# Gate-matrix one-hots in a Trainium2 block: two tokens side by side in place of eight

## Chip, core and metric

The kernel runs as one program on one core of a Trainium2 chip. The core has five engines with a queue each: TensorE (PE; its weight loads are shown apart as PEld), VectorE (DVE), ScalarE (ACT), GpSimd (POOL) and SyncE (SP), which here only issues DMAs. The metric is the device time of one execution in microseconds. A profile gives the span from the first to the last instruction of one execution.

## What is computed

The reference is one transformer block on 512 latent tokens of width 1024 (with 256 context tokens): two recurrent token mixers, a merge, and a product-key mixture of experts ("PEER"). Only the last part is touched:

```python
q = (t @ w_query).reshape(n_tok, P_HEADS, 2, P_DQ)
sc = jnp.einsum('thcd,hckd->thck', q, sub_keys)
s1, i1 = lax.top_k(sc[:, :, 0], P_TOPK)
s2, i2 = lax.top_k(sc[:, :, 1], P_TOPK)
cand = (s1[..., :, None] + s2[..., None, :]).reshape(n_tok, P_HEADS, P_TOPK * P_TOPK)
top_s, top_i = lax.top_k(cand, P_TOPK)
e1 = jnp.take_along_axis(i1, top_i // P_TOPK, axis=-1)
e2 = jnp.take_along_axis(i2, top_i % P_TOPK, axis=-1)
experts = (e1 * P_NKEYS + e2)
gates = jax.nn.softmax(top_s, axis=-1)
...
act = jax.nn.gelu(jnp.einsum('td,tkd->tk', tb, expert_u[eb])) * gb
return jnp.einsum('tk,tkd->td', act, expert_v[eb])
```

There are 8 heads with 16 picks each, so 128 experts per token, out of 128 x 128.

## The kernel before

**Two ways for the tokens.** The 512 tokens are four blocks of 128. Block 0 fetches its 128 experts per token by indirect DMA (helper `gather`: one gather of 128 rows of 4 KB and one VectorE step on it, 256 times in all). Blocks 1 to 3 go through all 16384 experts with dense matmuls: `side_u(e)` loads one tile of `u` (512 KB), splits it into a high and a low part (`whi` on ScalarE, `wlo` on GpSimd or VectorE) and makes 24 matmuls (lines 99 to 101 of `mm3`, 128 weights columns against 384 token columns, into `pS`); later the same is done with `v`, weighted by a dense gate matrix `G[token, e1, e2]`.

**The gate matrix.** `routing(b)` for b = 1, 2, 3 makes that matrix for 128 tokens. For each token the matrix is a product of two one-hot matrices over the 128 picks: `oh1[:, 0]` holds (e1 == column) and `oh2` holds (e2 == column) times the gate, the gate in two fp16 parts (z = 0, 1). Picks lie on partitions. The loop over `tg` (16 tokens) and `t8` (8 tokens) is one round per 8 tokens, 16 rounds per block, 48 in all. One round is:

- VectorE, line 1228: `oh1` = (iota == index) for both indices, 128 partitions x 2048 fp16;
- VectorE, line 1229: `oh2` = second half of `oh1` times the gate parts, 2048 fp16;
- TensorE, line 1235: 16 pairs of a weight load (128 columns of `oh1` or `oh2`) and a matmul over 128 columns, two per token, into two PSUM banks `pg_` of four tokens;
- ScalarE, line 1237: two evictions of 128x512 into `st`;
- SyncE, line 1238: per two rounds, 1 MB of `st` to DRAM (`GD`).

The lines of the operands before:

```python
sel = pR.tile([128, 2, 128], F16, name="sel", bufs=2)
oh1 = pR.tile([128, 2, 128, 8], F16, name="oh1", tag="oh", bufs=4)
oh2 = pR.tile([128, 2, 128, 8], F16, name="oh2", tag="oh", bufs=4)
V.tensor_tensor(oh1, twice(io8), over(sel, ts), op=OP.is_equal)
held[0] = V.tensor_tensor(oh2, twice(oh1[:, 1]), over(ghl, ts), op=OP.mult)
T.matmul(pg_[:, q_], oh1[:, 0, :, t], oh2[:, z, :, t], start=z == 0, stop=z == 1)
```

Tokens are the innermost dimension (8 fp16 = 16 bytes), so both TensorE operands of one token step 8 elements, 16 bytes, from one column to the next. VectorE's operand `sel` or `ghl` is a run of 8 elements that is read 128 times over.

**What sets the order.** The generators `routing(b)` and `us()` are woven by `weave` (15 steps of routing to 20 tiles of `u`), and the build then schedules the instructions of each engine by its own cost estimates, so a change of shapes can move instructions between their neighbours. All engines take their queue in order. The four buffers of tag `oh` are two rounds: `oh1` of a round can be written when the matmuls of the round two before are done. `wraw` has two buffers, `whi` and `wlo` three each, `gr` five, `gst` two. `held` ties each gather's VectorE step behind the last VectorE step of the stage. One block's work thus has an index stretch (top-k, no gate matmuls) and a gate stretch (16 rounds).

## Time and profile before

| | |
|---|---|
| device time, median of 3 runs | 3078.58 us (3072.75 to 3085.27) |
| span of the profiled execution | 3060.6 us |
| median less span | 18.0 us |
| busy share PE / DVE / ACT / POOL | 94% / 60% / 37% / 36% |
| three gate stretches | 109.6 + 108.3 + 107.0 = 324.9 us |

The page has the span of the profiled execution and no device time of its own for it; the 18.0 us are the distance of that span to the runs' median. The gate stretches run from the first one-hot of a block to its last gate matmul: 1744.6 to 1854.2, 1906.5 to 2014.8 and 2068.1 to 2175.1 us. [...] A matmul's shown length is longer than its distance to the next, since matmuls are pipelined; distances between starts are the measure.

### The profile page before, as it was taken

The page shows a single profiled execution, that of the slowest core. Times are in us where ns is not written, and L with a number is a line of the kernel's source. Part 1 is how long each engine was busy: PE and PEld are TensorE (multiplying, and loading weights), DVE is VectorE, ACT ScalarE, POOL GpSimd, SP SyncE. Part 2 cuts the span into 40 slices and gives each one's busy share as a digit, 9 for nine tenths or more (in the row PEclk, how much of TensorE's full clock was granted, in tenths as well). Part 3 has the DMA queues.
Part 4 walks back from the last instruction along what each step waited for, and adds up shares of the span by engine and source line. Part 5 has one row for each costly group of instructions (what it writes and reads, how often), then busy time and mean ns, then how long its engine had stood idle before and what let it go on. Part 6 is the DMA issues. An engine that isn't in the chain of part 4 may idle for free.

```text
span 3060.6 us, 40793 instructions
## 1 busy us (share of the span) xinstructions
PE 2875.4 (94%) x15664; PEld 2277.6 (74%) x15664; DVE 1848.8 (60%) x3273; ACT 1122.3 (37%) x1647; POOL 1100.0 (36%) x674
## 2 busy tenths in 40 slices
PE   6899999999999999999999799999999999999998
PEld 3777667766776666667788678787888888887776
DVE  6555455455453567734578957455577766666668
ACT  3433323333332555515223244434333333333333
POOL 2313223232220222200003625252466655655665
PEclk9999999999999989999999788898899999999999
DMA  5323223232232323326423656564788888878885
GB/s 204 98 67 90 67 70 95 75 86 77 83 83 68 112 81 104 100 89 204 158 92 109 199 184 207 185 212 155 252 289 283 294 279 273 291 280 286 285 279 195
DMA packets 243732, 507.92 MB, mean 166 GB/s; under 512 B 56736, under 2 KB 125760, under 8 KB 239440
## 3 DMA queue, kind: packets, MB, share of 16 engines
q1 hardware_dynamic: 206672, 371.07, 37.5%
q0 software_dynamic: 36864, 134.23, 12.4%
q8 instruction: 123, 2.02, 0.3%
q14 instruction: 73, 0.60, 0.1%
HBM read 440.37 MB, written 64.86 MB: 165 GB/s over the span
## 4 chain that ended last, share of the span: by engine, by line
PE 34%; DMA 10%; DVE 6%; issue 2%; ACT 2%; POOL 1%; SPq 0%; ACTq 0%; DVEq 0%; POOLq 0%
DMA wraw<-in_u_t 6%; PE pS L101 4%; PE pS L99 4%; PE pS L100 4%; PE oacc L100 3%; DMA wraw<-in_v_rows 3%; PE oacc L101 3%; PE oacc L99 3%; DVE wlo L95 2%; ACT whi L94 1%; PE pq L99 1%; PE pq L101 1%; PE pq L100 1%; DVE gscr L1098 1%; PE psc L1132 0%
## 5 line engine op out<-in xcount | busy, mean ns | idle before, releaser
L94 ACT CAST whi<-wraw 128x1024 fp32r<-128x1024 f32 x384 | 402.9, 1050 | 893.3 <-DMA wraw<-in_v_rows 225.8
L95 DVE TENSOR_TENSOR wlo<-wraw,whi 128x1024 fp32r<-128x1024 f32 x333 | 491.1, 1475 | 328.0 <-ACT whi L94 321.9
L99 PE MATMUL pS<-tTh,whi 128*128 128x384 f32 x1024 | 377.8, 369 | 36.1 <-ACT whi L94 24.3
L101 PE MATMUL pS<-tTh,wlo 128*128 128x384 f32 x1024 | 374.6, 366 | 10.7 <-POOL wlo L95 6.6
L100 PE MATMUL pS<-tTl,whi 128*128 128x384 f32 x1024 | 373.5, 365 | 0.0
L99 PE MATMUL oacc<-whi,ah 128*128 128x512 f32 x768 | 302.8, 394 | 16.1 <-ACT ah L1281 16.1
L100 PE MATMUL oacc<-wlo,ah 128*128 128x512 f32 x768 | 304.2, 396 | 2.7 <-DVE wlo L95 2.6
L101 PE MATMUL oacc<-whi,al 128*128 128x512 f32 x768 | 303.6, 395 | 0.9 <-DVE al L1282 0.9
L99 PE MATMUL pcl<-hTh,whi 128*128 128x512 f32 x704 | 301.1, 428 | 0.0
L1277 POOL TENSOR_TENSOR ag<-af,gread 128x384 f32<-128x384 f32 x128 | 224.4, 1753 | 211.8 <-DVE al L1282 201.1
L101 PE MATMUL pcl<-hTh,wlo 128*128 128x512 f32 x704 | 292.0, 415 | 0.0
L100 PE MATMUL pcl<-hTl,whi 128*128 128x512 f32 x704 | 290.9, 413 | 0.0
L99 PEld LDWEIGHTS pS<-tTh,whi 128*128 128x128 f32 x1024 | 215.4, 210 | 45.6 <-ACT whi L94 27.2
L95 POOL TENSOR_TENSOR wlo<-wraw,whi 128x1024 fp32r<-128x1024 f32 x51 | 125.8, 2469 | 313.5 <-ACT whi L94 219.8
L1095 POOL DMA_INDIRECT gr<-in_u_rows,eidx x128 | 178.7, 1396 | 142.9 <-DVE gscr L1098 101.2
L101 PEld LDWEIGHTS pS<-tTh,wlo 128*128 128x128 f32 x1024 | 214.4, 209 | 16.2 <-POOL wlo L95 7.9
L100 PEld LDWEIGHTS pS<-tTl,whi 128*128 128x128 f32 x1024 | 214.3, 209 | 3.3
L1095 POOL DMA_INDIRECT gr<-in_v_rows,eidx x128 | 191.6, 1497 | 67.1 <-DVE gacc L1102 46.9
L99 PEld LDWEIGHTS oacc<-whi,ah 128*128 128x128 f32 x768 | 146.2, 190 | 47.6 <-ACT ah L1281 18.8
L100 PEld LDWEIGHTS oacc<-wlo,ah 128*128 128x128 f32 x768 | 146.1, 190 | 35.1 <-DVE wlo L95 5.7
L101 PEld LDWEIGHTS oacc<-whi,al 128*128 128x128 f32 x768 | 145.9, 190 | 33.2 <-DVE al L1282 2.9
L1098 DVE SCALAR_TENSOR_TENSOR gscr<-gr,ttk 128x1024 bf16<-128x1024 f32 x128 | 169.5, 1324 | 0.7
(1197 smaller groups left out, 5462.5 us busy)
## 6 DMA issues: line engine op xcount, KB each, us to landing
wraw<-in_u_t SPq DMA_DIRECT2D x128, 512.0 KB, 4.4
wraw<-in_v_rows SPq DMA_DIRECT2D x128, 512.0 KB, 4.7
wraw<-in_w_c SPq DMA_DIRECT2D x88, 512.0 KB, 3.7
GD<-gst SPq DMA_DIRECT2D x24, 1024.0 KB, 4.2
gread<-GD SPq DMA_DIRECT2D x16, 1536.0 KB, 12.9
bw<-in_w_ada SPq DMA_DIRECT2D x64, 256.0 KB, 2.9
afD<-afx SPq DMA_DIRECT2D x56, 192.0 KB, 3.6
af<-afD SPq DMA_DIRECT2D x56, 192.0 KB, 4.7
```

The source lines that it names most:

```text
L94: S.copy(hi, raw)
L95: (eng or V).tensor_tensor(lo, raw, hi.bitcast(F32), op=OP.subtract)
L99: T.matmul(o, Lh, Rh, start=first, stop=False)
L100: T.matmul(o, Lh, Rl, start=False, stop=False)
L101: T.matmul(o, Ll, Rh, start=False, stop=last)
L1095: G.indirect_dma_start(out=r, out_offset=None, in_=A["u_rows" if i < NSEL else "v_rows"], in_offset=IndirectOffsetOnAxis(ap=eidx[:, n:n + ...
L1098: x = V.scalar_tensor_tensor(scr, r, 1.0, ttk, op0=OP.mult, op1=OP.mult, accum_out=gs[:, n:n + 1])
L1277: G.tensor_tensor(ag.rearrange("p (g t) -> p g t", t=GT), af.rearrange("p (g t) -> p g t", t=GT), gr[:, :, e % EG, :], op=OP.mult)
```

## The change

The innermost dimension of the one-hots goes from 8 tokens to 2. `oh1` and `oh2` are now [128, 8, 128, 2]: of the 8 slabs of `oh1`, 0 to 3 are e1 and 4 to 7 are e2 for token pairs; the slabs of `oh2` are the two gate parts. TensorE's operands step 2 elements (4 bytes) from column to column. `io8` becomes `io2` (256 elements in place of 1024); `sel` is stored per 8 tokens so that one operand covers e1 and e2, which ScalarE's copy writes in that order. `oh2`, which was one instruction of 2048 elements, becomes two of 1024. Comment lines are removed as well; that part of the diff is left out here.

```diff
-            io8 = pR.tile([128, 128, 8], F16, name="io8")
-            G.iota(io8, pattern=[[1, 128], [0, 8]], base=0, channel_multiplier=0, allow_small_or_imprecise_dtypes=True)
+            io2 = pR.tile([128, 128, 2], F16, name="io2")
+            G.iota(io2, pattern=[[1, 128], [0, 2]], base=0, channel_multiplier=0, allow_small_or_imprecise_dtypes=True)
...
-                sel = pR.tile([128, 2, 128], F16, name="sel", bufs=2)
+                sel = pR.tile([128, 16, 2, 8], F16, name="sel", bufs=2)
...
-                S.copy(sel, pt3[:, 0:2])
+                S.copy(sel.rearrange("p g z t -> p z g t"), pt3[:, 0:2].rearrange("p z (g t) -> p z g t", t=8))
...
-                def over(ap, ts):
-                    """[p, 2, t] -> [p, 2, 128, 8]"""
-                    return ap[:, :, None, ts].to_broadcast([128, 2, 128, 8])
-
-                def twice(ap):
-                    return ap[:, None].to_broadcast([128, 2, 128, 8])
+                def over(ap):
+
+                    n = ap.shape[1] // 2
+                    return ap.rearrange("p (t u) -> p t u", u=2)[:, :, None, :].to_broadcast([128, n, 128, 2])
...
-                        oh1 = pR.tile([128, 2, 128, 8], F16, name="oh1", tag="oh", bufs=4)
-                        oh2 = pR.tile([128, 2, 128, 8], F16, name="oh2", tag="oh", bufs=4)
-                        V.tensor_tensor(oh1, twice(io8), over(sel, ts), op=OP.is_equal)
-                        held[0] = V.tensor_tensor(oh2, twice(oh1[:, 1]), over(ghl, ts), op=OP.mult)
+                        oh1 = pR.tile([128, 8, 128, 2], F16, name="oh1", tag="oh", bufs=4)
+                        oh2 = pR.tile([128, 8, 128, 2], F16, name="oh2", tag="oh", bufs=4)
+                        V.tensor_tensor(oh1, io2[:, None].to_broadcast([128, 8, 128, 2]),
+                                        over(sel[:, (tg * GT + t8) // 8].rearrange("p z t -> p (z t)")),
+                                        op=OP.is_equal)
+                        for z in range(2):
+                            held[0] = V.tensor_tensor(oh2[:, 4 * z:4 * z + 4], oh1[:, 4:8], over(ghl[:, z, ts]),
+                                                      op=OP.mult)
...
-                                    T.matmul(pg_[:, q_], oh1[:, 0, :, t], oh2[:, z, :, t], start=z == 0, stop=z == 1)
+                                    T.matmul(pg_[:, q_], oh1[:, t // 2, :, t % 2], oh2[:, 4 * z + t // 2, :, t % 2],
+                                             start=z == 0, stop=z == 1)
```

The build also moves instructions. On TensorE, at the first two rounds of the first gate stretch (`oh_13688` and `oh_13689` are the first round's one-hots, `pg` its banks, `pS` the matmuls of `side_u`), before:

```order
L1235 MATMUL pg__13702<-oh_13689,oh_13688 128x128
L99 MATMUL pS<-tTh,whi 128x384
L100 MATMUL pS<-tTl,whi 128x384
L101 MATMUL pS<-tTh,wlo 128x384
L99 MATMUL pS<-tTh,whi 128x384
L100 MATMUL pS<-tTl,whi 128x384
L101 MATMUL pS<-tTh,wlo 128x384
L99 MATMUL pS<-tTh,whi 128x384
L100 MATMUL pS<-tTl,whi 128x384
L1235 LDWEIGHTS oh_13712
L1235 MATMUL pg__13716<-oh_13713,oh_13712 128x128
```

And now (line 1237 is the line that was 1235):

```order
L1237 MATMUL pg__13703<-oh_13689,oh_13688 128x128
L101 MATMUL pS<-tTh,wlo 128x384
L99 MATMUL pS<-tTh,whi 128x384
L1237 LDWEIGHTS oh_13713
L1237 MATMUL pg__13718<-oh_13714,oh_13713 128x128
L1237 LDWEIGHTS oh_13713
L1237 MATMUL pg__13728<-oh_13714,oh_13713 128x128
L101 MATMUL pS<-tTh,wlo 128x384
L99 MATMUL pS<-tTh,whi 128x384
L1237 LDWEIGHTS oh_13713
L1237 MATMUL pg__13718<-oh_13714,oh_13713 128x128
```

Most rounds are now split: their first two pairs (the first pair of each bank) stand two or three `pS` matmuls ahead of the other fourteen. The number of gate pairs and of `pS` matmuls is the same.

On VectorE, at the same place (`io` is the iota, `gscr` the step on a gathered row, `pos`, `top_s` and `c` belong to block 2's top-k), before:

```order
L1228 TENSOR_TENSOR oh_13688<-io_11931,sel 128x2048
L1213 SCALAR_TENSOR_TENSOR ghl<-pt_13678,ghl 128x128
L1161 MAX top_s<-c_14537 128x8
L1229 TENSOR_TENSOR oh_13689<-oh_13688,ghl 128x2048
L1228 TENSOR_TENSOR oh_13712<-io_11931,sel 128x2048
L1162 MAX_INDEX pos<-top_s,c_14537 128x8
L1229 TENSOR_TENSOR oh_13713<-oh_13712,ghl 128x2048
L1098 SCALAR_TENSOR_TENSOR gscr,gs<-gr,ttk 128x1024
L1228 TENSOR_TENSOR oh_13775<-io_11931,sel 128x2048
```

And now:

```order
L1226 TENSOR_TENSOR oh_13688<-io_11931,sel 128x2048
L1213 SCALAR_TENSOR_TENSOR ghl<-pt_13678,ghl 128x128
L1230 TENSOR_TENSOR oh_13689<-oh_13688,ghl 128x1024 x2
L1226 TENSOR_TENSOR oh_13713<-io_11931,sel 128x2048
L1161 MAX top_s<-c_14553 128x8
L1230 TENSOR_TENSOR oh_13714<-oh_13713,ghl 128x1024 x2
L1098 SCALAR_TENSOR_TENSOR gscr,gs<-gr,ttk 128x1024
L1226 TENSOR_TENSOR oh_13777<-io_11931,sel 128x2048
```

The sequence stays; the gate product is two instructions, and small top-k steps move by a place. The gathers on GpSimd, the evictions on ScalarE and the stores and loads on SyncE are the same in number, some by one to four places earlier or later. Outside the routing of blocks 1 to 3 the order is the same, but for the size of the iota.

## Rows read from the trace of the kernel before

**Rows 1.** The page: its first lines, with the busy time of each engine over the span.

```profile
span 3060.6 us, 40793 instructions
PE 2875.4 (94%) x15664; PEld 2277.6 (74%) x15664; DVE 1848.8 (60%) x3273; ACT 1122.3 (37%) x1647; POOL 1100.0 (36%) x674
```

**Rows 2.** The window view of six stretches: the three gate stretches, the two index stretches between them, and the first part of the loop over `v` behind. Columns: from:to, length, busy us and (count) of PE, PEld, DVE, ACT, POOL, then granted TensorE clock, busy share of the DMA engines, GB/s.

```profile
1744.60:1854.20 109.60, 106.81 (x449) 83.53 (x450) 63.88 (x85) 48.97 (x52) 28.20 (x18) 0.80 0.50 174
1854.20:1906.50 52.30, 48.56 (x267) 47.78 (x266) 40.94 (x112) 19.81 (x27) 31.87 (x16) 0.96 0.72 245
1906.50:2014.80 108.30, 108.22 (x449) 84.75 (x450) 55.06 (x58) 45.20 (x48) 26.95 (x16) 0.80 0.48 168
2014.80:2068.10 53.30, 49.06 (x269) 48.07 (x268) 28.98 (x29) 16.60 (x24) 30.52 (x16) 0.96 0.75 243
2068.10:2175.10 107.00, 106.96 (x447) 83.62 (x448) 56.74 (x57) 45.35 (x49) 29.83 (x18) 0.83 0.48 167
2190.00:2480.00 290.00, 274.12 (x1349) 247.47 (x1349) 207.10 (x254) 94.25 (x131) 182.58 (x116) 0.98 0.84 292
```

**Rows 3.** The window view of the gate matmuls of line 1235 alone, first gate stretch: length, PE busy and count, PEld busy and count, clock, DMA.

```profile
1744.60:1854.20 109.60, 62.62 (x256) 36.21 (x256) 0.80 0.50 174
```

**Rows 4.** The timeline of TensorE around the second and around the fourth round: start, length, instruction. Each round is 16 gate pairs, shown as two rows of 8.

```profile
1753.01 0.52 PE L99 MATMUL pS<-tTh,whi 128*128 128x384 f32 x1
1753.33 0.52 PE L100 MATMUL pS<-tTl,whi 128*128 128x384 f32 x1
1753.65 2.08 PE L1235 MATMUL pg__13716<-oh,oh 128*128 128x128 f16 x8
1755.55 2.04 PE L1235 MATMUL pg__13726<-oh,oh 128*128 128x128 f16 x8
1757.23 0.68 PE L101 MATMUL pS<-tTh,wlo 128*128 128x384 f32 x1
...
1760.51 0.33 PE L101 MATMUL pS<-tTh,wlo 128*128 128x384 f32 x1
1760.68 0.34 PE L99 MATMUL pS<-tTh,whi 128*128 128x384 f32 x1
1760.86 2.08 PE L1235 MATMUL pg__13779<-oh,oh 128*128 128x128 f16 x8
1762.77 2.04 PE L1235 MATMUL pg__13789<-oh,oh 128*128 128x128 f16 x8
1764.45 0.54 PE L100 MATMUL pS<-tTl,whi 128*128 128x384 f32 x1
```

**Rows 5.** The window view of those two rounds; columns as in rows 2, the clock is the third number from the end.

```profile
1753.70:1757.10 3.40, 3.40 (x16) 2.21 (x16) 1.76 (x4) 1.06 (x1) 1.27 (x1) 0.50 0.57 156
1760.90:1764.30 3.40, 3.40 (x16) 2.20 (x16) 0.00 (x0) 1.05 (x1) 0.00 (x0) 1.00 0.34 135
```

**Rows 6.** Waits in the first gate stretch, longest first: who waited for whom, us in total, times, longest.

```profile
DVE oh L1228 <- PE pg__14171 L1235: 5.1, 1, 5.1
DVE oh L1228 <- PE pg__13997 L1235: 4.9, 1, 4.9
ACT gst L1237 <- PE pg__13863 L1235: 4.8, 1, 4.8
```

**Rows 7.** The timeline of TensorE at the first scores of the top-k, 8 dense fp32 pairs of 128 weight columns against 128 columns (4 bytes from column to column), and the window view that holds them.

```profile
1557.34 1.05 PE L1132 MATMUL psc<-sk,qT__12005 128*128 128x128 f32 x8
...
1557.30:1558.20 0.90, 0.90 (x10) 0.86 (x9) 0.00 (x0) 0.89 (x1) 0.00 (x0) 1.00 0.02 9
```

**Rows 8.** The view of weight loads and matmuls of single lines: count, then ns least/median/most of one.

```profile
L1235 PEld LDWEIGHTS <-oh x768: 142/146/173, 1745.9 to 2174.5; 128*128 128x128 f16 x192
...
L1132 PEld LDWEIGHTS psc<-sk,qT__12005 x8: 188/192/192, 1557.1 to 1558.0; 128*128 128x128 f32 x8
L1132 PE MATMUL psc<-sk,qT__12005 x8: 271/275/275, 1557.3 to 1558.1; 128*128 128x128 f32 x8
```

**Rows 9.** The same view for VectorE steps: the two one-hot steps; then 1024 fp32 elements with one operand a row of 16 read 64 times and the other one element read 16 times on end (line 1188); then a 512-element step that writes 64 elements apart (line 1346) and its twin that writes densely (line 1349).

```profile
L1228 DVE TENSOR_TENSOR oh<-io,sel x48: 1208/1225/2872, 1744.7 to 2161.3; 128x2048 f16<-128x2048 f16 x48
L1229 DVE TENSOR_TENSOR oh<-oh,ghl x48: 1200/1224/3411, 1746.1 to 2163.4; 128x2048 f16<-128x2048 f16 x48
L1188 DVE TENSOR_TENSOR eq<-iot,fa x8: 1216/1218/3414, 1667.6 to 2013.4; 128x1024 f32<-128x1024 f32 x8
L1346 DVE SCALAR_TENSOR_TENSOR oT<-pt_f,hnw,gb x8: 1083/1132/1153, 1107.7 to 1352.7; 128x512 f32<-128x512 f32 x8
L1349 DVE SCALAR_TENSOR_TENSOR oT<-quad,gnw,ga x8: 750/751/753, 265.3 to 1015.7; 128x512 f32<-128x512 f32 x8
```

**Rows 10.** Groups of VectorE instructions in the first gate stretch: count, busy us, mean ns of one, idle before. The last is a step of 128 elements.

```profile
L1229 DVE TENSOR_TENSOR oh<-oh,ghl 128x2048 f16<-128x2048 f16 x16 | 23.7, 1480 | 0.0
L1228 DVE TENSOR_TENSOR oh<-io,sel 128x2048 f16<-128x2048 f16 x16 | 19.6, 1223 | 34.9 <-PE pg__14171 L1235 5.1 <-PE pg__13997 L1235 4.9 <-PE pg__13789 L1235 4.7
L1213 DVE SCALAR_TENSOR_TENSOR ghl<-pt,ghl 128x128 f16<-128x128 f32 x1 | 0.3, 283 | 0.0
```

## The prediction

> **What bounds the kernel now.** I read the page first: TensorE is busy 94% of the span [rows 1]. That alone says little, so the next view is the window view of the stage that the change touches, cut at the gate stretches. In them TensorE is busy 322.0 of 324.9 us, while VectorE has 58.6 us per stretch on average, ScalarE 46.5, GpSimd 28.3, and the DMA moves 170 GB/s where it moves 243 to 292 in the stretches around [rows 2]. So in the gate stretches TensorE is the bound and nothing else is near. The waits agree: the longest ones there are VectorE's one-hots and ScalarE's evictions waiting for gate matmuls [rows 6], and of VectorE's idle time 34.9 us lies before the one-hots in the first stretch [rows 10].
>
> What TensorE does there is 256 gate pairs of 449 matmuls [rows 2, 3], so 193 are `pS`. A round of 16 gate pairs takes, from its first start to the start of the next other matmul, 1757.23 - 1753.65 = 3.58 us, and 1764.45 - 1760.86 = 3.59 us [rows 4]. [...] A time that does not move with the clock is not TensorE's own rate: it is 224 ns per pair whatever the clock, and the reading of the operands is what is left to set it. Beside it, eight dense fp32 pairs of the same 128 by 128 shape at full clock take (1.05 - 0.275) / 7 = 0.111 us each [rows 7, 8], though their weight load is the longer one, 192 ns against 146 [rows 8]. They step 4 bytes from column to column; the gate operands step 16.
>
> So a stretch of 108.3 us is 16 x 3.58 = 57.3 us of gates and 51.0 us for 193 `pS`, 0.264 us each. The `pS` are 0.175 us apart at full clock (1760.68 to 1760.86 and 1760.51 to 1760.68 are 0.18 and 0.17) and 0.32 at half clock (1753.01, 1753.33, 1753.65) [rows 4]. The clock over the gate stretches is 0.80 to 0.83, in the index stretches, where the same `pS` run without gates, 0.96 [rows 2]: TensorE falls back behind slow rounds.
>
> **The change part by part.** The **gate matmuls** now step 4 bytes, as the dense fp32 rows do. Their price is not in this trace. The upper bound is 0.111 us, the dense fp32 pair [rows 7]; the lower is 128 columns at the rate of `pS`, 0.175 x 128 / 384 = 0.058 us [rows 4]. The weight load is shorter than the fp32 one [rows 8], so I take the middle, 0.085 us: 256 x 0.085 = 21.8 us per stretch (14.9 to 28.4), where 57.3 stood. All of that lies on the path, since TensorE is the bound.
>
> [...]
>
> The **`pS` matmuls** are not touched, but their clock may be: 193 x 0.175 = 33.8 us per stretch if it is granted in full, 51.0 us if it stays as it is. TensorE alone then needs 21.8 + 33.8 = 55.6 us, or 72.8 with the clock as now, and 79.4 with the dearer pair as well.
>
> The split of a round into 2 and 14 pairs adds a switch per round; a switch shows above within the 3.58 us, so it is priced at nothing beyond the bounds. What could be queued behind it is the `pS` work: if the first two pairs wait for one-hots, the fourteen and the `pS` behind them wait too. VectorE works up to two rounds ahead, and between the end of a round and the start of the second one after it TensorE has about 20 `pS` and one round, 20 x 0.175 + 16 x 0.085 = 4.9 us, against 2.4 + 0.15 us of one-hots and at most two or three other steps of 1.2 us. That is covered with little to spare.
>
> The **one-hot steps** on VectorE: 2048 fp16 elements take 1.225 us [rows 9], half the time per element of 1024 fp32 in 1.218, so they run two elements at a time today, with `sel` in runs of 8. Runs of 2 are no row of this trace. The nearest is line 1188, where one operand is a single 4-byte element read 16 times on end: 1.218 us for 1024, full rate for fp32 [rows 9]. Two fp16 tokens are one such 4-byte word read 128 times on end, so I take the step to stay at 1.225. Bounds: not faster, since elements and operation are the same; at the dear end one element at a time or worse, which the first and the third rival price. `oh2` in two halves pays one more fixed part. From 1024 and 128 elements, 1.218 and 0.283 us [rows 9, 10], the slope is 1.04 ns and the fixed part 0.15 us; 16 x 0.15 = 2.4 us per stretch. VectorE: 58.6 + 2.4 = 61.0 us. This hides behind whatever ends the stretch, and costs 7 us in all if nothing does.
>
> The iota on GpSimd, 256 elements for 1024, and ScalarE's three copies into `sel` lie under other work, once or three times in the program: nothing. The moved gathers, stores and loads keep their number and neighbours: nothing beside the bounds.
>
> **What is late next.** A gate stretch moves 170 GB/s x 108.3 us = 18.4 MB. At the rate of the index stretches, 244 GB/s, that takes 75.4 us; at the rate of the loop behind, 292, it takes 63 us [rows 2]. So the candidates per stretch are TensorE 55.6 to 72.8 (79.4), VectorE 61, DMA 63 to 75. I take **75 us**: the DMA at the rate it reaches between the stretches, which also holds TensorE with its clock unchanged. Gain 108.3 - 75 = 33.3 us, three times, 100 us. The index stretches and the loop over `v` run the same instructions at rates that the DMA sets already; they start earlier and give nothing back, since gathers are placed by count of steps, not by time. Span 3060.6 - 100 = 2960.6; with the 18.0 us between span and median, **2978.6 us**. Ends of this case: 64 us per stretch (DMA at 292) gives 3078.6 - 133 = 2946; 86 us (the dearer TensorE sum, 79.4, with the 8% of waiting that the index stretches show, 48.56 of 52.30 busy [rows 2]) gives 3078.6 - 67 = 3012.
>
> **The rivals.**
>
> *VectorE loses its pairs.* If runs of 2 break the reading of two elements at a time, `oh1` costs 2048 x 1.04 + 150 = 2.28 us and `oh2` twice 1.218; per round 4.72 in place of 2.45, per stretch 16 x 2.27 = 36 us, so 58.6 + 36.3 = 95 us with VectorE as the bound, 103 with 8% of waiting. Gain 40 to 16 us: 3039 to 3063, say 3051. For it: the run is as short as it can be, and this trace has only runs of 8. Against it: the repeated 4-byte element of line 1188 costs nothing [rows 9].
>
> [...]
>
> *TensorE is not faster.* If the 224 ns belong to fp16, or to a load and a matmul of operands from the same tiles, and not to the step, the gates stay at 57.3 us, VectorE's 7 us hide, and the time stays at 3079. For it: no fp16 pair with another step is in the trace. Against it: the same shape in fp32 takes half of it at full clock [rows 7], and only reading explains a time that ignores the clock [rows 4, 5].
>
> *Slower: VectorE pays for every word apart.* One-hots without pairs, and each element dearer as in the step that writes 64 elements apart: 1132 against 751 ns for 512, 0.74 ns more per element [rows 9]. Then a round costs 4.72 + 4096 x 0.74 / 1000 = 7.75 us, 5.3 more than now; per stretch 58.6 + 85 = 143 us, 35 more than now, three times: 3183. It decides from 3.1 us more per round (50 us between VectorE's 58.6 and the stretch's 108.3, by 16). For it only that VectorE has such steps; against it that the new operands lie in dense rows.
>
> **How the numbers follow.** Forecast case 0.70 (2946 to 3012) with 0.03 for a time below it; VectorE without pairs or in part 0.13 (3003 to 3063); TensorE no faster 0.09 (3079); VectorE dearer by the element 0.05 (3183). Leaving out the last two and the ends, the range is 2942 to 3054. A measurement of this kernel can tell 0.5%, 15 us, from no change, so faster is below 3063: 0.70 + 0.03 + 0.11 = 0.84; within it 0.09 + 0.02 = 0.11; slower 0.05.
>
> **What would show it.** Right: a round of 16 gate pairs in 1.0 to 1.8 us, not 3.58; gate stretches of 64 to 86 us with the DMA above 210 GB/s; the `oh1` step at 1.2 us and each half of `oh2` near 0.68; a clock above 0.83 in the stretches; the loop over `v` of the same length. Wrong: `oh1` near 2.3 us (first rival); rounds still at 3.5 us (second); a gate stretch with VectorE busy throughout (first and third). If the stretches shrink and the time does not, the loop behind took it back, and the step that failed is the one that says it gives nothing back.

## The result, and the profile after

The changed kernel takes **2955.09 us** (median of 4 runs, 2946.93 to 2969.11), the kernel before 3075.87 beside it (3072.75 to 3085.27): a ratio of 0.961, 95% interval 0.957 to 0.965, or 120.8 us. The forecast was 2978.6 with a range of 2942 to 3054. The profiled execution has a span of 2945.2 us where 3060.6 stood, 115.4 us less. The page's first lines, which answer to [rows 1]:

```profile
span 2945.2 us, 40847 instructions
PE 2725.1 (93%) x15664; PEld 2177.9 (74%) x15664; DVE 1886.2 (64%) x3321; ACT 1110.6 (38%) x1647; POOL 1117.1 (38%) x674
```

The window view of the same six stretches, which answers to [rows 2]: three gate stretches, the two index stretches between them and the first part of the loop over `v`. Columns: from:to, length, busy us and (count) of PE, PEld, DVE, ACT, POOL, then granted clock of TensorE as a share of full speed, DMA share, GB/s. The second and third gate stretch are cut at their first gate matmul, here and in [rows 2]; the first one-hots of those blocks lie in the index stretch ahead.

```profile
1751.60:1816.20 64.60, 55.39 (x453) 50.35 (x454) 64.24 (x85) 41.16 (x48) 28.43 (x14) 0.93 0.78 279
1816.20:1876.90 60.70, 48.66 (x263) 46.79 (x262) 54.51 (x128) 22.64 (x31) 36.31 (x20) 0.94 0.71 225
1876.90:1941.80 64.90, 56.69 (x453) 51.36 (x454) 63.12 (x66) 42.28 (x49) 29.78 (x14) 0.92 0.82 278
1941.80:1999.10 57.30, 51.55 (x268) 49.98 (x268) 33.21 (x36) 16.39 (x24) 33.55 (x17) 0.91 0.72 229
1999.10:2063.20 64.10, 54.16 (x451) 49.28 (x451) 63.27 (x67) 40.24 (x47) 30.34 (x15) 0.95 0.73 252
2075.00:2365.00 290.00, 272.46 (x1334) 245.57 (x1333) 203.55 (x249) 93.39 (x130) 182.34 (x113) 0.97 0.83 289
```

The three gate stretches now take 193.6 us in place of 324.9, 131.3 less. The index stretches take 118.0 in place of 105.6, 12.4 more. The first gate stretch begins 7.0 us later (1751.6 against 1744.6; the code ahead of it is the same), and from the last gate matmul to the end it is 882.0 us against 885.5, 3.5 less. Together -131.3 + 12.4 + 7.0 - 3.5 = -115.4, the difference of the spans. The last two terms are no more than one execution differs from another: a second profile of the changed kernel, with nearly the same span (2944.9 us), began its first gate stretch at 1743.9 us and took 892.0 us behind the last gate matmul, with gate stretches of 64.6, 64.0 and 65.7 us.

In the gate stretches the full column has moved. Before it was PE's; now DVE is busy 64.24 of 64.60, 63.12 of 64.90 and 63.27 of 64.10 us, and PE 54 to 57. The DMA moves 252 to 279 GB/s, more than in the index stretches (225 and 229). By these columns VectorE ends these stretches; an added step, below, tests it.

The timeline of TensorE at one round of the first stretch (start, length), which answers to [rows 4], and one line each of the weight loads and matmuls (count, ns least/median/most), which answer to [rows 8]:

```profile
1764.59 0.23 PE L1237 MATMUL pg__13807<-oh,oh 128*128 128x128 f16 x1
1764.66 0.22 PE L1237 MATMUL pg__13817<-oh,oh 128*128 128x128 f16 x1
...
1765.30 0.58 PE L1237 MATMUL pg__13807<-oh,oh 128*128 128x128 f16 x7
1765.72 0.56 PE L1237 MATMUL pg__13817<-oh,oh 128*128 128x128 f16 x7
...
L1237 PEld LDWEIGHTS <-oh x768: 96/97/149, 1752.9 to 2062.9; 128*128 128x128 f16 x192
L1237 PE MATMUL pg__13718<-oh,oh x8: 218/218/233, 1758.0 to 1758.9; 128*128 128x128 f16 x8
```

Seven pairs lie between the starts of the last two timeline rows: 0.42 us, 0.060 us per pair, where 0.224 stood; the granted clock between 1764.5 and 1766.1 us was 1.00. VectorE's one-hot steps, in the same view as [rows 9], then their groups in the first stretch, as in [rows 10]:

```profile
L1226 DVE TENSOR_TENSOR oh<-io,sel x48: 1205/1218/3805, 1751.7 to 2058.2; 128x2048 f16<-128x2048 f16 x48
L1230 DVE TENSOR_TENSOR oh<-oh,ghl x96: 666/684/2885, 1753.0 to 2060.0; 128x1024 f16<-128x1024 f16 x96
...
L1230 DVE TENSOR_TENSOR oh<-oh,ghl 128x1024 f16<-128x1024 f16 x32 | 24.7, 812 | 0.0
L1226 DVE TENSOR_TENSOR oh<-io,sel 128x2048 f16<-128x2048 f16 x16 | 21.7, 1355 | 0.0
L1098 DVE SCALAR_TENSOR_TENSOR gscr<-gr,ttk 128x1024 bf16<-128x1024 f32 x9 | 15.4, 1707 | 0.0
```

The idle column says as much as the busy one: before, 34.9 us of VectorE's idle time lay ahead of the one-hots [rows 10], now 0.0. The waits of that stretch have turned round as well: where VectorE waited for gate matmuls [rows 6], TensorE now waits for VectorE. One thing has to be set right here: the lines of [rows 6] are not the longest of that view. Waits of GpSimd and ScalarE lead it before and after, as in the first line of each view below, the view of before in the first block; those engines were busy 28 and 49 of 109.6 us before, and 28 and 41 of 64.6 us after.

```profile
POOL wlo L95 <- ACT whi L94: 67.9, 6, 25.0
```

```profile
POOL wlo L95 <- ACT whi L94: 16.0, 4, 10.8
...
PEld L1237 <- DVE oh L1230: 8.3, 8, 2.4
...
PE pg__13693 L1237 <- DVE oh L1230: 5.3, 1, 5.3
PEld L1237 <- DVE oh L1226: 4.8, 1, 4.8
```

The last two lines are the wait for the first one-hots of the block; the eight waits of the line above them lie ahead of later rounds.

One thing in these rows the prediction had not asked: the medians are 1218 and 684 ns, the means 1355 and 812, the longest 3805 and 2885. Some VectorE steps are three to four times as long as the rest.

### The profile page after: what moved, and what is told of

Read it like the earlier page. It is cut to its first block, busy times and chain, and to the rows that moved or that the text cites. A ratio compares the mean times of both kernels' runs of the same rounds, so it can differ in the third digit from the quotient of the medians.

```text
span 2945.2 us, 40847 instructions
## 1 busy us (share of the span) xinstructions
PE 2725.1 (93%) x15664; PEld 2177.9 (74%) x15664; DVE 1886.2 (64%) x3321; ACT 1110.6 (38%) x1647; POOL 1117.1 (38%) x674
## 4 chain that ended last, share of the span: by engine, by line
PE 20%; DMA 14%; DVE 12%; issue 3%; ACT 2%; POOL 2%; SPq 0%; ACTq 0%; DVEq 0%; POOLq 0%
DMA wraw<-in_u_t 6%; DMA wraw<-in_v_rows 6%; DVE wlo L95 3%; PE oacc L100 3%; PE oacc L101 3%; PE oacc L99 3%; DVE oh L1230 2%; PE pS L101 2%; PE pS L99 2%; PE pS L100 2%; DVE gscr L1098 2%; ACT whi L94 2%; DVE oh L1226 2%; PE pq L101 1%; PE pq L99 1%
## 5 line engine op out<-in xcount | busy, mean ns | idle before, releaser
L99 PE MATMUL pS<-tTh,whi 128*128 128x384 f32 x1024 | 360.6, 352 | 42.2 <-ACT afx L994 23.2
L101 PE MATMUL pS<-tTh,wlo 128*128 128x384 f32 x1024 | 358.5, 350 | 10.6 <-POOL wlo L95 6.8
L100 PE MATMUL pS<-tTl,whi 128*128 128x384 f32 x1024 | 356.8, 348 | 0.0
L1095 POOL DMA_INDIRECT gr<-in_u_rows,eidx x128 | 191.9, 1499 | 143.3 <-DVE gscr L1098 121.7
L99 PEld LDWEIGHTS pS<-tTh,whi 128*128 128x128 f32 x1024 | 201.9, 197 | 51.6 <-ACT afx L994 27.2
L1095 POOL DMA_INDIRECT gr<-in_v_rows,eidx x128 | 190.3, 1487 | 62.6 <-DVE gacc L1102 42.5
L101 PEld LDWEIGHTS pS<-tTh,wlo 128*128 128x128 f32 x1024 | 201.6, 197 | 14.4 <-POOL wlo L95 8.1
L100 PEld LDWEIGHTS pS<-tTl,whi 128*128 128x128 f32 x1024 | 201.9, 197 | 2.1
L1098 DVE SCALAR_TENSOR_TENSOR gscr<-gr,ttk 128x1024 bf16<-128x1024 f32 x128 | 183.5, 1434 | 0.6
```

The costliest lines, as they stand in the source:

```text
L99: T.matmul(o, Lh, Rh, start=first, stop=False)
L100: T.matmul(o, Lh, Rl, start=False, stop=False)
L101: T.matmul(o, Ll, Rh, start=False, stop=last)
L1095: G.indirect_dma_start(out=r, out_offset=None, in_=A["u_rows" if i < NSEL else "v_rows"], in_offset=IndirectOffsetOnAxis(ap=eidx[:, n:n + ...
L1098: x = V.scalar_tensor_tensor(scr, r, 1.0, ttk, op0=OP.mult, op1=OP.mult, accum_out=gs[:, n:n + 1])
```

## The experiments

Three questions were open. **Why is a gate pair cheaper**: the step of an operand or something else, which operand, and does the price grow with the step or jump at some step? **What ends a gate stretch now**: VectorE, or the DMA whose rate the forecast took? **Why are some VectorE steps long**, and is that worth time?

### The step of the operands

**Four tokens side by side** (8 bytes from column to column), the rest as in the changed kernel:

```diff
-                    return ap.rearrange("p (t u) -> p t u", u=2)[:, :, None, :].to_broadcast([128, n, 128, 2])
+                    return ap.rearrange("p (t u) -> p t u", u=4)[:, :, None, :].to_broadcast([128, n, 128, 4])
...
-                        oh1 = pR.tile([128, 8, 128, 2], F16, name="oh1", tag="oh", bufs=4)
+                        oh1 = pR.tile([128, 4, 128, 4], F16, name="oh1", tag="oh", bufs=4)
```

> Four tokens side by side: TensorE's operands step 8 bytes, VectorE's runs are of 4. Theory A (a column costs more only where every column falls in a 16-byte line of its own): a round of 16 gate pairs takes 1.0 to 1.1 us as with 4 bytes, gate stretches 64 to 66 us, time within 10 us of the changed kernel, 2955 us. Rival B (the price grows with the bytes stepped over): about 0.11 us a pair, 1.8 us a round, TensorE 62 us per stretch beside VectorE's 64, so stretches of 66 to 72 us and 2960 to 2980 us. The one-hot steps keep 1.22 and 0.68 us in both.

Measured: 2959.77 us, ratio 0.9638 (0.9602 to 0.9674). Timeline of TensorE at the same round, and the weight loads:

```profile
1763.98 1.00 PE L1237 MATMUL pg__13807<-oh,oh 128*128 128x128 f16 x7
1764.80 1.01 PE L1237 MATMUL pg__13817<-oh,oh 128*128 128x128 f16 x7
...
L1237 PEld LDWEIGHTS <-oh x768: 111/117/147, 1750.0 to 2064.5; 128*128 128x128 f16 x192
```

0.82 us for seven pairs, 0.117 each, at a granted clock of 1.00: twice the price of the 4-byte step, half that of the 16-byte step. So the price grows with the step; two columns within 16 bytes are not free. The weights step 8 bytes here as well; that they do not set this price follows from the next two runs. The time hardly shows it: 256 x 0.117 = 30 us of gates and some 34 us of `pS` are 64 us, an estimate, which is what VectorE needs anyway; the stretches are 66 to 67 us from first to last gate matmul, where the changed kernel has 62 to 65.

**Only the moving operand in pairs, and only the weights in pairs.** Each keeps the other operand at a 16-byte step, by making the two halves of `oh1` in two VectorE steps (`ow` is the half that serves as weights). The matmul of the first, then of the second:

```diff
-                                    T.matmul(pg_[:, q_], oh1[:, t // 2, :, t % 2], oh2[:, 4 * z + t // 2, :, t % 2],
+                                    T.matmul(pg_[:, q_], ow[:, :, t], oh2[:, 4 * z + t // 2, :, t % 2],
                                              start=z == 0, stop=z == 1)
...
-                                    T.matmul(pg_[:, q_], oh1[:, t // 2, :, t % 2], oh2[:, 4 * z + t // 2, :, t % 2],
+                                    T.matmul(pg_[:, q_], ow[:, t // 2, :, t % 2], oh2[:, z, :, t],
                                              start=z == 0, stop=z == 1)
```

> Only the moving operand (oh2) has two tokens side by side; the weights (the e1 half of oh1) step 16 bytes as before, and oh1 is built by two steps of 1024 elements. If the stream of the moving operand set the 224 ns per pair, pairs take 0.06 to 0.09 us, weight loads still 146 ns, gate stretches about 64 + 2 to 66 + 2 us, time 2955 to 2970 us. Rival (the weight load set it): pairs stay at 0.22 us and the time at 3070 to 3085 us.

> Only the weights have two tokens side by side; the moving operand steps 16 bytes as before, and both one-hot steps are two of 1024 elements. If the moving stream set the 224 ns, weight loads fall to 97 ns and pairs stay at 0.22 us: 3065 to 3085 us. Rival (the weight load set it): pairs at 0.06 to 0.09 us and 2955 to 2970 us. If both did, pairs land between and so does the time.

Measured: 2963.97 us (0.9646, 0.9611 to 0.9681) with the moving operand alone; 3076.43 (1.0013, 0.9989 to 1.0037) with the weights alone. Weight loads and timeline of the first, then of the second:

```profile
L1243 PEld LDWEIGHTS <-oh x768: 141/145/174, 1750.4 to 2064.7; 128*128 128x128 f16 x192
...
1765.34 0.66 PE L1243 MATMUL pg__13813<-oh,oh 128*128 128x128 f16 x7
1765.84 0.60 PE L1243 MATMUL pg__13823<-oh,oh 128*128 128x128 f16 x7
```

```profile
L1243 PEld LDWEIGHTS <-oh x768: 96/118/148, 1753.6 to 2189.0; 128*128 128x128 f16 x192
...
1768.75 1.76 PE L1243 MATMUL pg__13787<-oh,oh 128*128 128x128 f16 x7
1770.33 1.78 PE L1243 MATMUL pg__13797<-oh,oh 128*128 128x128 f16 x7
```

With the old weights, whose load still shows 145 ns, a pair costs 0.50 / 7 = 0.071 us; with the old moving operand and quicker weight loads, 1.58 / 7 = 0.226 us, the price of before. The stream of the moving operand set the price, and with it all but 9 us of the gain. Those 9 us have another likely source in this run, its extra VectorE step per round: 48 x (2 x 0.684 - 1.218) = 7 us, an estimate.

**One token per slab** (dense columns). VectorE's operand is then one element repeated 128 times, which is the first rival's case of a lost pair:

```diff
-                    return ap.rearrange("p (t u) -> p t u", u=2)[:, :, None, :].to_broadcast([128, n, 128, 2])
+                    return ap[:, :, None].to_broadcast([128, n, 128])
...
-                        oh1 = pR.tile([128, 8, 128, 2], F16, name="oh1", tag="oh", bufs=4)
+                        oh1 = pR.tile([128, 16, 128], F16, name="oh1", tag="oh", bufs=4)
```

> One token on its own: TensorE's operands are dense (2 bytes), VectorE's second operand is one element read 128 times on end. If VectorE needs a run of at least two fp16 to take two elements at a time, the 2048-element step takes 2.28 us and each half of the gate product 1.22 us, VectorE has 64 + 36 = 100 us per gate stretch and the time is 3050 to 3065 us with gate pairs at 0.06 us. Rival (pairs do not depend on the run): steps stay at 1.22 and 0.68 us and the time within 10 us of 2955 us.

Measured: 3035.74 us, 0.988 (0.9845 to 0.9915). VectorE's steps, then the window of the first gate stretch, in which DVE is busy all of the time:

```profile
L1226 DVE TENSOR_TENSOR oh<-io,sel x48: 2272/2282/4483, 1756.5 to 2148.1; 128x2048 f16<-128x2048 f16 x48
L1230 DVE TENSOR_TENSOR oh<-oh,ghl x96: 1198/1215/3411, 1758.9 to 2152.6; 128x1024 f16<-128x1024 f16 x96
```

```profile
1756.50:1862.00 105.50, 78.06 (x543) 70.90 (x542) 105.50 (x93) 48.27 (x57) 46.24 (x17) 0.84 0.55 191
```

2.282 us for 2048 elements is the 2.28 that the prediction worked out for a lost pair. A run of one loses it, a run of two does not (1.218). The gate stretches are 99.4, 111.1 and 102.8 us from first to last gate matmul, near the 103 that the rival worked out; but the two index stretches between them are 48.8 and 34.4 us where 52.3 and 53.3 stood, and so the time lies under the rival's 3039 to 3063 and under the 3050 of the expectation. Long gate stretches take in work of VectorE that otherwise stands between them.

### What ends a gate stretch

**One more one-hot step per round**, written to a tile nobody reads, in the changed kernel (shown) and likewise in the kernel before:

```diff
+                        dup = pR.tile([128, 8, 128, 2], F16, name="dup", bufs=1)
+                        V.tensor_tensor(dup, io2[:, None].to_broadcast([128, 8, 128, 2]),
+                                        over(sel[:, (tg * GT + t8) // 8].rearrange("p z t -> p (z t)")),
+                                        op=OP.is_equal)
```

> The changed kernel with one more one-hot step of 2048 elements per round on VectorE, written to a tile that nobody reads. Theory (VectorE is what ends the gate stretches now): the step is paid in full, 48 x 1.15 to 1.22 us = 55 to 59 us, stretches of 82 to 84 us, time 3005 to 3020 us. Rival (the DMA at its rate, or TensorE, ends them and VectorE only looks full): much of it hides, under 30 us more, time below 2985 us.

> The same added step in the kernel before. Theory (TensorE's strided reading ends the gate stretches there, VectorE at 58.6 of 108.3 us): 58.6 + 18 us still fit, the time stays within 10 us of 3074 us. Rival (the one-hots are on the path of a round, since only two rounds are buffered): 20 to 58 us more, 3094 to 3132 us.

Measured: 3009.16 us for the changed kernel with it (0.9787, 0.9752 to 0.9822), 54.1 us more than without; the steps alone are 48 x 1.218 = 58.5 us. In the profiles 44.0 us of them lie in the gate stretches, which are 235.5 us from first to last gate matmul against 191.5. The kernel before with it: 3085.95 (1.0021, 1.0001 to 1.0041), 9.1 us over the kernel before beside it, an interval just clear of no change; its gate stretches did not grow (318.8 us against 322.0), and where the 9 us lie was not shown. So VectorE ends the stretches of the changed kernel and had room in those of before.

**The gate product as one step of 2048**, by storing `ghl` per 8 tokens as `sel` is; this takes the second fixed part back out (`e2` is the e2 half of `oh1` read twice, `g4` the gate parts of 8 tokens; their lines are left out):

```diff
-                        for z in range(2):
-                            held[0] = V.tensor_tensor(oh2[:, 4 * z:4 * z + 4], oh1[:, 4:8], over(ghl[:, z, ts]),
-                                                      op=OP.mult)
...
+                        held[0] = V.tensor_tensor(oh2.rearrange("p t c u -> p (t c u)"), e2, g4, op=OP.mult)
```

> The changed kernel with the gate product again as one step of 2048 elements (ghl stored per 8 tokens like sel). Theory (VectorE ends the stretches): one fixed part per round less, 0.09 to 0.15 us x 48 = 4 to 7 us, time 2948 to 2952 us where the changed kernel has 2955 to 2957. Rival (the split costs nothing, or another engine ends the stretches): no difference, within 2 us.

Measured: 2951.35 us, 0.9587 (0.9567 to 0.9607). On one chip with the changed kernel:

> The same kernel as the run with the gate product in one step, now on the same chip as the changed kernel and in five rounds. If the 48 saved fixed parts (0.15 us each, 7.2 us in all) lie on the path, it is 5 to 8 us faster than the changed kernel on the same chip; if they lie in VectorE's idle time it is within 2 us of it.

> The changed kernel itself, for comparison on the same chip: 2947 to 2962, as before; stretches of 62 to 66 us.

2954.97 (0.9598, 0.9565 to 0.963) and 2956.81 (0.961, 0.9576 to 0.9643). In both pairs of profiles its three gate stretches, counted from the first one-hot of each block, are 6 us shorter in sum (193.3 and 193.9 us against 199.3 and 200.0). The times are 2 to 4 us apart, within the intervals: the stretches became shorter, and whether the whole did is neither shown nor excluded.

**The merged form with all low parts of `u` in this stage on GpSimd**, so as to relieve VectorE of the 17 that it makes there:

```diff
-        Uh, Ul = wload(A["u_t"][e], [128, KD, 128], eng=G if e < NS + LA and (e % UP or e < UV) else V)
+        Uh, Ul = wload(A["u_t"][e], [128, KD, 128], eng=G if e < NS + LA else V)
```

> As merged, and all low parts of the u tiles of this stage on GpSimd, none on VectorE (about 17 steps of 1.25 us off VectorE, 17 of 2.4 us more on GpSimd, which is busy 30 of 64 us per stretch). Theory (VectorE ends the stretches): some 9 of those steps lie in gate stretches, 11 us less, less what longer VectorE steps beside a busy GpSimd give back: time 2935 to 2950 us. Rival (GpSimd's steps hold VectorE up by as much as they take off it, or the DMA at 279 GB/s is the next bound at once): 2948 to 2960 us.

Measured: 2973.19 us, 0.9648 (0.9622 to 0.9675), slower than without it; neither side had this. Groups of the `oh1` step between 1700 and 2130 us, merged, then with the low parts on GpSimd:

```profile
L1227 DVE TENSOR_TENSOR oh<-io,sel 128x2048 f16<-128x2048 f16 x48 | 66.7, 1389 | 6.0 <-ACT sel L1212 5.8 <-PE pg__13789 L1240 0.2
```

```profile
L1227 DVE TENSOR_TENSOR oh<-io,sel 128x2048 f16<-128x2048 f16 x48 | 80.6, 1679 | 39.7 <-ACT sel L1212 37.6 <-PE pg__14171 L1240 1.4 <-PE pg__15287 L1240 0.4
```

VectorE lost work and its remaining steps grew, 1389 to 1679 ns on average; the gate stretches are 198.8 us from first to last gate matmul against 183.6. The 37.6 us of idle time lie outside them, 14.6 and 23.0 us in the index stretches ahead of blocks 2 and 3. That led to the third question.

### VectorE beside GpSimd

The timeline of the changed kernel at two long steps, VectorE's and GpSimd's side by side (start, length; the bracket is the idle time before):

```profile
1757.79 3.41 DVE L1226 TENSOR_TENSOR oh<-io,sel 128x2048 f16<-128x2048 f16 x1
1773.80 3.43 DVE L1098 SCALAR_TENSOR_TENSOR gscr<-gr,ttk 128x1024 bf16<-128x1024 f32 x1
```

```profile
1757.23 2.88 POOL L95 TENSOR_TENSOR wlo<-wraw,whi 128x1024 fp32r<-128x1024 f32 x1 [6.40 <-PE pS L101]
1772.81 3.34 POOL L95 TENSOR_TENSOR wlo<-wraw,whi 128x1024 fp32r<-128x1024 f32 x1 [10.79 <-ACT whi L94]
```

GpSimd's steps end at 1760.11 and 1776.15, VectorE's at 1761.20 and 1777.23, that is 1.09 and 1.08 us later: about one undisturbed VectorE step after GpSimd's end. By these times the long VectorE step is one that waited for GpSimd's, and the wait is shown as busy. The two are no chance pair. Between 1700 and 2100 us the changed kernel has 205 steps of three kinds (48 of `oh1`, 96 halves of `oh2`, 61 on gathered rows). 25 of them are over 10% longer than the median of their kind; each of the 25 overlaps a GpSimd tensor step, and each ends 0.55 us (the halves) or 1.08 to 1.09 us (the others) after a GpSimd step ends. In three of them GpSimd's step is shown to begin 0.3 to 0.4 us later than VectorE's, so the shown starts do not always tell which goes first. TensorE feels it: its longest wait for a half of `oh2` in the first stretch, 2.4 us, ends with one that took 2.71 us (1779.68 to 1782.39).

Two runs test the price.

**GpSimd's low-part steps left out:**

```diff
+        if nolo:
+            return hi, hi
...
-        Uh, Ul = wload(A["u_t"][e], [128, KD, 128], eng=G if e < NS + LA and (e % UP or e < UV) else V)
+        Uh, Ul = wload(A["u_t"][e], [128, KD, 128], eng=G if e < NS + LA and (e % UP or e < UV) else V,
+                       nolo=UE <= e < NS + LA and (e % UP or e < UV))
```

> The changed kernel without GpSimd's low-part steps: for the 45 or so tiles of u that GpSimd splits from tile 2 to tile 67, the low part is left out and the high part is used in its place as weights (so that part of the split of u is left out of the result). VectorE's own instructions are the same in number and shape. Theory: VectorE ends the gate stretches, and GpSimd's concurrent steps make its steps longer (up to 3.4 us where 1.2 is the median). Then the one-hot step's mean falls from 1.35 to 1.22 to 1.27 us, the half products from 0.84 to 0.67 to 0.72, the gathered-row step from 1.64 to 1.2 to 1.4; the stretches fall from 64 to 54 to 59 us, and the time to 2920 to 2940. Rival: the long steps come from something else (the DMA's writes, ScalarE's copies, or the recording), the means stay at 1.35 and 0.84, the stretches at 62 to 65 and the time at 2945 to 2958.

Measured: 2888.12 us, 0.939 (0.9353 to 0.9428), 67 us under the changed kernel: the theory's side, but below its 2920 to 2940. The `oh1` step, then groups between 1650 and 2100 us, then two gate stretches with the index stretch between them (here the second is cut at its first one-hot):

```profile
L1229 DVE TENSOR_TENSOR oh<-io,sel x48: 1214/1219/1227, 1733.4 to 1985.9; 128x2048 f16<-128x2048 f16 x48
```

```profile
L1101 DVE SCALAR_TENSOR_TENSOR gscr<-gr,ttk 128x1024 bf16<-128x1024 f32 x80 | 100.1, 1251 | 0.3
L1233 DVE TENSOR_TENSOR oh<-oh,ghl 128x1024 f16<-128x1024 f16 x96 | 61.9, 686 | 0.8
L1229 DVE TENSOR_TENSOR oh<-io,sel 128x2048 f16<-128x2048 f16 x48 | 58.6, 1220 | 6.9 <-ACT sel L1214 5.7 <-PE pg__13760 L1240 1.1
```

```profile
1733.40:1790.20 56.80, 54.45 (x458) 50.30 (x459) 54.45 (x96) 41.50 (x49) 11.58 (x8) 0.94 0.86 316
1790.20:1838.90 48.70, 44.62 (x248) 43.95 (x248) 40.97 (x123) 21.19 (x30) 18.13 (x12) 0.96 0.80 274
1838.90:1892.70 53.80, 53.80 (x470) 49.87 (x470) 53.35 (x71) 40.50 (x49) 13.64 (x9) 1.00 0.89 327
```

The spread of the `oh1` step is gone: 1214 to 1227 ns, where the changed kernel has 1205 to 3805. The DMA reaches 316 and 327 GB/s in these stretches, so the 244 of the forecast was never a limit there. Cut at the first gate matmul like the others, the first index stretch is 50.9 us in place of 60.7, with the same 128 VectorE instructions in it. This run drops GpSimd's work and also the wait of each tile for its low part; the next one drops neither.

**The low parts that GpSimd makes from tile 2 on, 49 in all, on VectorE**, nothing left out:

```diff
-        Uh, Ul = wload(A["u_t"][e], [128, KD, 128], eng=G if e < NS + LA and (e % UP or e < UV) else V)
+        Uh, Ul = wload(A["u_t"][e], [128, KD, 128], eng=G if e < UE else V)
```

> The changed kernel with the low parts of u from tile 2 on (among them the 45 tiles or so that GpSimd splits) on VectorE, nothing left out: 1.22 us more on VectorE for each, and no GpSimd tensor step of this line beside it. Theory: GpSimd's and VectorE's two-operand steps run one after the other, never at once, so a low part on GpSimd costs VectorE the rest of a step of 2.5 to 3.4 us when the two meet, which is more than the 1.22 us of doing it itself. Then the one-hot steps fall to 1.22 and 0.69 us on average, the gate stretches from 64 to 58 to 62 us (VectorE 54 as without the low parts, and 5 to 6 tiles of 1.22 us), the index stretches by some us, and the time is 2910 to 2940. Rival: the 45 steps of 1.22 us, 55 us in all, cost VectorE as much as the collisions do (some 47 us above the medians), and the time is 2947 to 2965, as the changed kernel. The other rival: the gain without the low parts came from a shorter way of each tile to its matmuls; then VectorE's queue makes that way longer and the time is above 2965.

Measured: **2911.97 us**, 0.9464 (0.9431 to 0.9497), 43 us under the changed kernel and the fastest complete version here. Its `oh1` and `oh2` steps, then its three gate and two index stretches:

```profile
L1226 DVE TENSOR_TENSOR oh<-io,sel x48: 1210/1218/1224, 1738.2 to 2012.0; 128x2048 f16<-128x2048 f16 x48
...
L1230 DVE TENSOR_TENSOR oh<-oh,ghl x96: 667/683/696, 1741.8 to 2015.0; 128x1024 f16<-128x1024 f16 x96
```

```profile
1738.20:1800.10 61.90, 59.23 (x490) 53.72 (x489) 59.20 (x85) 43.29 (x50) 12.38 (x8) 0.97 0.84 296
1800.10:1852.40 52.30, 44.98 (x234) 43.02 (x233) 47.36 (x124) 19.21 (x27) 20.07 (x12) 0.93 0.76 257
1852.40:1909.50 57.10, 56.43 (x480) 51.04 (x481) 56.27 (x83) 42.35 (x50) 12.91 (x8) 1.00 0.87 311
1909.50:1957.00 47.50, 42.56 (x229) 40.34 (x229) 44.94 (x88) 18.07 (x25) 20.27 (x11) 0.96 0.78 267
1957.00:2016.80 59.80, 59.23 (x498) 53.99 (x499) 58.93 (x75) 44.31 (x52) 12.91 (x8) 1.00 0.82 293
```

VectorE got more work and the kernel became faster. In the three gate stretches of the changed kernel its steps lie 39 us in sum above the medians of their kinds, beside 18 low parts on GpSimd: 2.2 us for each, where a low part of its own costs it 1.22. The 43 us are 14.8 in the gate stretches (178.8 against 193.6), 18.2 in the index stretches (99.8 against 118.0) and 13.4 by an earlier start of the first one, less 3.9 behind (42.5 by spans). The two profiles of the changed kernel differ from each other by 8 us in the start and 10 us behind, so these two parts are rough. In the second index stretch VectorE was busy only 33.2 of 57.3 us before the move, so longer VectorE steps do not explain the 9.8 us gained there; a shorter way of a tile to its matmuls may, and was not tested. TensorE and VectorE now fill the gate stretches alike.

## Why the prediction was right, and where its sum was off

**What bounded the kernel, and why** was right. The price of a round, 3.58 us at a granted clock of 0.50 and 3.59 at 1.00 [rows 4, 5], was laid to the reading of an operand; the runs show that it goes with the step of the moving one (0.071 us a pair with that operand alone at 4 bytes, 0.226 with the weights alone), and the second rival (TensorE no faster) is refuted.

**The gate pair** was taken at 0.085 us from bounds of 0.058 and 0.111 and measured 0.060. The right row was the lower bound's, `pS` by columns; the fp32 pair, 0.111 us, has the same step and a dearer load (192 ns [rows 8] against 97), and was not the measure. 256 x 0.060 = 15.4 us per stretch in place of 21.8. The clock over the stretches rose from between 0.80 and 0.83 to between 0.92 and 0.95. At a clock of 1.00 TensorE's own need would be 15.4 + 197 x 0.175 = 50 us, an estimate, under the 55.6 of the forecast, and the view shows it busy 54 to 57. That the clock falls behind slow rounds, as the prediction has it, is not the whole of it: with one token per slab the pairs were quick as well (0.057 us), and the clock in the first gate stretch was 0.84, with TensorE busy 78 of 105.5 us.

**VectorE keeps its pairs**: right, 1.218 us, and 0.684 for each half. The first and third rival are refuted for a run of two, and the run of one shows that the first rival's price was worked out well. For the 3003 us at the low end of "VectorE without pairs or in part" no run shows a term: the `oh1` step has a median of 1.218 us with two tokens side by side and of 2.282 with one, and no run had a median between. One of the prediction's signs of being wrong did come, VectorE busy throughout a gate stretch, which it had put down to these two rivals. Neither is the cause: the steps kept their median length, and the stretch had come down to VectorE's own work and its waits. The signs of being right came as well, but for the round of 16 pairs, which at 0.060 us a pair is 0.96 us, just under the 1.0 to 1.8.

**What is late next** is the term that was mis-sized. The prediction listed TensorE, VectorE at 61 and the DMA at 63 to 75 us per stretch, and took 75, because the DMA reached 244 GB/s in the index stretches. But that rate was what the work of those stretches asked for, not what the DMA could give: after the change it is 252 to 279 GB/s in the gate stretches, and 316 to 327 without GpSimd's steps. VectorE ended them, at 64.5 us on average: 10.5 less than taken, 31.5 us over three stretches. Its own estimate of 61.0 stood 2.5 us under the 63.5 us it was busy. That the time fell into the range all the same is in part luck: the stretches came out at its low end, 64 us, for another reason than the DMA, and the next error ran the other way.

**"Give nothing back"** was wrong by 15.9 us in this profile, and that hid half of the other error: 12.4 us in the index stretches, 7.0 by a later first stretch, less 3.5 behind. So 100 + 31.5 - 15.9 = 115.6 us, the 115.4 of the spans but for rounding. In the second profile of the changed kernel it is 14.9 us: 9.1 in the index stretches, 6.5 behind, less 0.7 by an earlier first stretch. So only the 9 to 12 us in the index stretches stand in both.

In the first index stretch VectorE has more to do, 128 instructions against 112 in [rows 2]: without the one-hot steps, the gate stretch in front holds 37 in place of 53. Its steps are longer too: the same 128 instructions stand in 50.9 us without GpSimd's low parts, in 60.7 with them. In the second index stretch VectorE is busy 33.2 of 57.3 us, so it does not end that one. The waits of TensorE name ScalarE's evictions of `pS` (9.6 and 5.8 us in the two stretches, 0.9 and 4.0 before), and ScalarE's high parts waited for the loads of their tiles (20.8 and 24.9 us, 12.4 and 21.1 before). Which of these lengthens the index stretches was not tested.

**The 18.0 us between span and median** were 9.9 for the changed kernel (2955.1 less 2945.2). These 8.1 us and the 15.4 by which the spans fell further than 100 are the 23.5 us between the forecast and the result.

**The cover named for the halves of `oh2`** ("costs 7 us in all if nothing does") was gone: VectorE ends the stretches. Its price is 32 x 684 - 16 x 1224 ns = 2.3 us per stretch, as worked out, but putting it back brought 6 us in the gate stretches of the profiles and 2 to 4 us in the times, which the runs could not tell from nothing.

**What was missed** stood in the rows: longest values of 2872 and 3411 ns beside medians of 1225 [rows 9], and a mean of 1480 [rows 10]. While TensorE was the bound, those waits of VectorE for GpSimd lay in its idle time, where 58.5 us of added steps cost 9. From means with and without GpSimd's steps they come to 0.131 x 48 + 0.193 x 96 + 0.386 x 61 = 48 us over the stage of the changed kernel, whose groups between 1700 and 2100 us are:

```profile
L1098 DVE SCALAR_TENSOR_TENSOR gscr<-gr,ttk 128x1024 bf16<-128x1024 f32 x61 | 99.9, 1637 | 0.2
L1230 DVE TENSOR_TENSOR oh<-oh,ghl 128x1024 f16<-128x1024 f16 x96 | 80.5, 879 | 0.8
L1226 DVE TENSOR_TENSOR oh<-io,sel 128x2048 f16<-128x2048 f16 x48 | 64.8, 1351 | 5.9 <-ACT sel L1211 5.9
```

## What to carry to other kernels

Where a matmul's distance to the next ignores the granted clock, as the 0.224 us of a pair did here at 0.50 and at 1.00, look at the step of its moving operand, and choose a layout that suits both readers: two fp16 side by side was short enough for TensorE (0.060 us a pair) and long enough for VectorE (1.218 us a step). When the bound of a stretch falls, list what is next by what each engine needs there; a DMA rate seen in another stretch can be what was asked for there, and not a limit, as the 244 GB/s were, where 316 to 327 came later. And before an engine becomes the next bound, compare the mean of its steps with their median: the gap here, 1351 ns against 1218 for the `oh1` step, was waiting for GpSimd that hid in VectorE's busy time, and moving GpSimd's work onto the busy engine was a gain of 43 us.

## What the runs showed of the hardware

- The price of an fp16 pair of 128 by 128 columns goes with the step of the moving operand: 0.060 us at 4 bytes, 0.117 at 8 (the weights at the same step), 0.224 to 0.226 at 16. With the weights at 16 bytes and the moving operand at 4 it is 0.071.
- At dense columns (2 bytes) a pair took 0.057 us in a round of the run with one token per slab (starts at 1781.67 and 1782.07 us), next to 0.060 at 4 bytes.
- A VectorE step on 2048 fp16 takes 1.218 us with an operand of two elements repeated 128 times, and 2.282 with one element repeated.
- Beside GpSimd's two-operand steps, 25 of 205 VectorE steps of the changed kernel were over 10% longer than the median of their kind, up to 3.87 us for a step on a gathered row (median 1.217) and 3.81 for an `oh1` step (1.218), each ending a fixed 0.55 or 1.08 to 1.09 us after such a GpSimd step; 21 others that overlap one kept their length (at most 1.25 us). In each of the two runs without GpSimd's low parts, all 48 `oh1` steps took 1.210 to 1.227.
